# One row tile and two columns through the memory features' tile, with regrouped splits and a shared softmax scaling

## The chip, the cores and the metric

The kernel runs on one core of a Trainium2 chip. The metric is the device time of one execution in microseconds. The engines are TensorE (PE; its weight loads are PEld), VectorE (DVE), ScalarE (ACT), GpSimd (POOL) and SyncE (SP), which here only issues DMAs. Each engine works through a list of its own, in order.

## The reference

One layer of a streaming encoder over a prompt of 2048 rows and 128 sample rows (8 streams of 16), width 1024. The rows are RMS-normalised and projected once; three groups of heads read the result, each result is gated, and one projection merges them:

```python
def _rmsnorm(x, g):
    xf = xf * lax.rsqrt(jnp.mean(xf * xf, axis=-1, keepdims=True) + EPS)
    return (xf * g.astype(jnp.float32)).astype(x.dtype)
...
    qa, ka, va, ga, qb, kb, vb, gb, qm, gm = _project(yp, g_pre[l], w_in[l])
    oa = _band_attention(...)      # A: 6 heads, own chunk of 64 rows and 8 chunks before
    ob = _band_attention(...)      # B: 6 query heads on 2 key heads, own chunk and 2 before, with sinks
    om = _attn_core(...)           # M: 4 heads into 256 memory tokens
    yp = _merge(yp, oa, ga, ob, gb, om, gm, w_out[l], g_post[l])
...
def _merge(x, oa, ga, ob, gb, om, gm, w_out, g_post):
    o = jnp.concatenate([oa * jax.nn.silu(ga), ob * jax.nn.silu(gb), om * jax.nn.silu(gm)], axis=-1) @ w_out
    return x + _rmsnorm(o, g_post)
```

The sample rows do the same with cached keys and values. The new keys and values are outputs too.

## The kernel before

**Precision.** A float32 product is made of three products of a rounded part and a residual: ACT rounds a value (`split`, L238; `load_w`, L157; `split_mixed`, L961), DVE or POOL subtracts to get the residual (L239, L158, L962), and TensorE does three passes. So each weight tile (128x1024, through `wraw` to `whl`) costs a DMA, an ACT pass and a DVE or POOL pass, and every tile that a matmul reads does likewise.

**Groups.** The prompt is worked in four groups of 512 rows (g = 0 to 3); group 0 carries the 128 sample rows as well. Each group has two lanes of steps that are interleaved by hand-set costs: a dense lane (`DENSE`) and an attention lane (`ATTENTION`).

- `V`, `K`, `Pa`, `Pb`: projections of values, keys, and of query, key and gate of a pair of heads (`project_T`, L217, with 128x512 moving; `project_N`, L230, with 128x256 moving).
- `N0`: `next_scales(g + 1)`, the RMS factors of the next group's rows. `row_scales` loads four tiles of 128 rows (L175) and squares each in place on ACT (L176) with a running sum; `row_factors` turns the four factors into a 128x512 tile by small matmuls (L187), kept in `rsn`. The row tiles come from the pool tag "x", which has two buffers, and which the samples' cached values (`vta`, `vtb`), the residual rows `xr` and the gains use too.
- `L0`: `load_rows(g + 1)` loads the next group's rows by columns (eight of 128x512), scales each (L194, DVE) and splits it (L238 on ACT, L239 on DVE for even and POOL for odd columns) into `xn`. For group 1 each column is a tile of its own under the tag "xk", two buffers, 256 KB a load (L199). For later groups the columns from 2 on come in pairs (L479).
- `Q0`, `Q1`: query and gate of the next group's memory heads. They read all eight columns in order.
- `O0` to `O3`: the output projection of the group before, in quarters. `O0` first splits the gated features of each row tile (`split_mixed`, L961 on ACT and L962 on DVE) into `mixhl`.
- `F0`: `finish`, the last norm and the residual rows (L546, L547, L548).
- `M0`, `M1`, `Aa0` to `Aa2`, `Ab0` to `Ab2` and, in group 0, `Sa`, `Sb`: the attention of two memory heads, two A heads, two B heads, and of the samples. A head's part is `weigh` (scores, row minimum, exponential, reciprocal, scaling of the exponentials) and `combine` (transposes L277, `split`, the product with the values L290, `merge` L297 and L298, and after the second head `gate`, L688 on POOL).

**Features.** `mo` holds 8 feature columns of 128 for each of 5 row tiles: 0 to 2 from A, 3 to 5 from B, 6 and 7 from M. From group 1 on the memory heads' results (6 and 7) go into `mom`, a separate tile of 128 x 2 x 4 x 128, since `mo` still holds the group before. In group 0 `mom` is not written. Feature 2 comes from `Aa2`, the last attention step of each group.

**Order.** Python code emits instructions in the order of the two lanes. The framework then fixes each engine's list when the program is built: it allots buffers and takes what is ready first by a timeline that it works out from expected durations. On the chip these lists are not reordered. `tc.issue_after(last["w"])` keeps a DMA behind the latest weight load in SP's list.

Of the kernel before, what the change touches and what calls it, by code (L numbers as in the profile page):

```python
# [9 lines left out]
F32 = mybir.dt.float32  # L10
# [3 lines left out]
ALU = mybir.AluOpType  # L14
# [4 lines left out]
D = 1024  # L19
KB = D // 128  # L20
# [45 lines left out]
def encoder_step(ctx, tc, x_p, x_s, xT0, xT, mem, memT, wt, wm, g_pre, g_mem, g_post, rel_rev, sink,  # L66
# [3 lines left out]
    pe, act, dve, pool, sp = nc.tensor, nc.scalar, nc.vector, nc.gpsimd, nc.sync  # L70
# [4 lines left out]
    xp = ctx.enter_context(tc.tile_pool(name="xp", bufs=2))  # L75
# [14 lines left out]
    mo = cst.tile([128, 5, KB, 128], F32, name="mo")  # L90
# [7 lines left out]
    mom = cst.tile([128, 2, 4, 128], F32, name="mom")  # L98
# [14 lines left out]
    mixhl = region(0, 5, 2, KB, 128)  # L113
# [33 lines left out]
    last = {}  # L147
# [18 lines left out]
        dve.tensor_scalar(rstd[:, :n], ss[:, :n], 1.0 / D, EPS, ALU.mult, ALU.add)  # L166
        pool.tensor_tensor(rstd[:, :n], rstd[:, :n], expo[:, :n], ALU.pow)

    def row_scales(rows):

        n = len(rows)
        st = stp.tile([128, 16], F32, tag="nst", name="nst", bufs=3)
        for i, src in enumerate(rows):
            xt = xp.tile([128, D], F32, tag="x", name="xt")
            sp.dma_start(out=xt, in_=src)  # L175
            act.activation(xt, xt, AF.Square, accum_out=st[:, i:i + 1])  # L176
        rms_scale(st, n, st[:, 8:16])
        return st[:, 8:8 + n]

    def row_factors(rstd, n):  # L180

        rb = p_mm.tile([128, 512], F32, tag="mm", name="rb") if n == 4 else p_s.tile([128, 1024], F32, tag="s", name="rb")
        dg = xp.tile([128, 640], F32, tag="xk", name="dg", bufs=2)
        for i in range(n):
            d = dg[:, i * 128:(i + 1) * 128]
            dve.tensor_scalar(d, ident, rstd[:, i:i + 1], None, ALU.mult)
            pe.matmul(rb[:, i * 128:(i + 1) * 128], ones, d, start=True, stop=True)  # L187
        return rb
# [268 lines left out]
    def group_rows(g):  # L457
        return [x_p[g * GR + i * 128:g * GR + (i + 1) * 128] for i in range(4)] + ([x_s] if g == 0 else [])

    def next_scales(g):  # L460
        rb = row_factors(row_scales(group_rows(g)), 4)
        act.activation(rsn, rb, AF.Copy)

    def zero_rows(q):

        for h in range(2):
            pool.memset(q[64 - 64 * h:128 - 64 * h, 2 + h].bitcast(F32), 0.0)

    def load_rows(g):
        if g == 1:  # L470
            zero_rows(qslots[2])
        t = {}

        def column(k):
            if g == 1 or k in (0, 1):
                return loaded(xT[g - 1, :, k], 512)
            if k % 2 == 0:
                t[0] = xp.tile([128, D], F32, tag="x", name="xk2")
                sp.dma_start(out=t[0].rearrange("p (k r) -> p k r", k=2), in_=xT[g - 1, :, k:k + 2])  # L479
            return t[0][:, 512 * (k % 2):512 * (k % 2) + 512]  # L480

        scaled(rsn, column, gpre, xnT[1], 512)
# [40 lines left out]
    def gains():  # L523
        t = xp.tile([128, D], F32, tag="x", name="gpost")
        sp.dma_start(out=t, in_=g_post.partition_broadcast(128))
        return t, stp.tile([128, 32], F32, tag="pst", name="pst", bufs=2)
# [112 lines left out]
    for g in range(NG):  # L639
# [53 lines left out]
        def attn_m(pr, q, Q, G):  # L693
            f = 6 + pr
            held = {}

            def weigh(h):
                s = p_s.tile([128, 1024], F32, tag="s", name="sm")
                st = stp.tile([128, 16], F32, tag="st", name="stm")
                for i in range(4):  # L700
                    scores(s, q, h, i * 128, [(i * 256, mK[:, pr], 0, 256)])
                dve.tensor_reduce(st[:, 0:4], s.rearrange("p (a b) -> p a b", b=256), AX.X, ALU.min)
                held[h] = []
                for i2 in range(2):
                    sb = sbp.tile([128, 640], F32, tag="sb", name="sbm")
                    for i in (2 * i2, 2 * i2 + 1):
                        act.activation(sb[:, (i % 2) * 256:(i % 2) * 256 + 256], s[:, i * 256:(i + 1) * 256], AF.Exp,
                                       bias=st[:, i:i + 1], scale=-1.0, accum_out=st[:, 4 + i:5 + i])
                    dve.reciprocal(st[:, 8 + 2 * i2:10 + 2 * i2], st[:, 4 + 2 * i2:6 + 2 * i2])
                    for i in (2 * i2, 2 * i2 + 1):  # L710
                        c = sb[:, (i % 2) * 256:(i % 2) * 256 + 256]
                        dve.tensor_scalar(c, c, st[:, 8 + i:9 + i], 0.5, ALU.mult, ALU.mult)
                    held[h].append(sb)
                yield 950

            def combine(h):
                if h == 0:
                    held["sums"] = cp_.tile([128, 512], F32, tag="sums", name="sums")
                o = p_o.tile([128, 512], F32, tag="o", name="om")
                for i2 in range(2):  # L720
                    pt = transposed_p([held[h][i2][:, i * 256 + j * 128:i * 256 + (j + 1) * 128]
                                       for j in range(2) for i in range(2)])
                    yield 440
                    attend(o, [(mV[:, pr, j, 128 * h:128 * h + 128], pt, 256 * j, 256, 256 * i2) for j in range(2)],
                           i2 == 0)
                    yield 470
                merge(o, h, 0, held["sums"], 512)
                if h:
                    gate(f, 0, 512, held["sums"], G)

            return [(weigh(h), combine(h)) for h in range(2)]


# [226 lines left out]
        def split_mixed(dst, i, fs, src):  # L960
            act.activation(dst[:, i, 0, fs], src, AF.Copy)  # L961
            dve.tensor_tensor(dst[:, i, 1, fs], src, dst[:, i, 0, fs].bitcast(F32), ALU.subtract)  # L962

        def out_quarter(c):

            nrt = 5 if g == 1 else 4
            if c == 0:
                turn["m"] = 1
                for i in range(nrt):
                    if g == 1:  # L970
                        split_mixed(mixhl, i, slice(0, KB), mo[:, i])
                    else:
                        split_mixed(mixhl, i, slice(0, 6), mo[:, i, :6])
                        split_mixed(mixhl, i, slice(6, KB), mom[:, :, i])
                kept["post"] = gains()
            ws = [weights("o", c, r) for r in range(2)]
            for i in range(nrt):
                yield from project_out(ws, c, i, *kept["post"])
            if c == 3:
                turn["m"] = 0  # L980
# [15 lines left out]
        def dense():  # L996
            for step in DENSE[g].split():
                yield after(step)
                what, j = step[:-1], int(step[-1])
                if what == "O":  # L1000
                    yield from out_quarter(j)
                elif what == "E":
                    yield from early_quarters()
                elif what == "V":
                    vsm.extend((yield from block_v(vslots[2 * j:2 * j + 2], j)))
                elif what == "K":
                    kept["ksm"] = yield from block_k(3, ks[3], bkT, bkTs, 128)
                    if g:
                        pool.tensor_copy(keys[:, :, 0:128], bctx[0].bitcast(F32))
                elif what == "N":  # L1010
                    next_scales(g + 1)
                elif what == "L":
                    load_rows(g + 1)
                elif what == "X":
                    load_ctx(j)
                elif what == "C":
                    kept["bctx"] = keep_context()
                elif what == "F":
                    finish(g - 1, [4] if j else range(4), kept["post"][1])
                elif what == "Q":  # L1020
                    q, Q = yield from block_q(g + 1, 6 + j)
                    new_qg.append((q, Q, (yield from block_g(g + 1, 6 + j))))
                elif what == "Pa":
                    pa[j] = yield from project_a(j, ks[j], vslots[j])
                elif what == "Pb":
                    pb[j] = yield from project_b(j)
                done.add((g, step))
# [46 lines left out]
        while any(lanes):  # L1074
            ready = [lanes[k] is not None and done.issuperset(waits[k]) for k in range(2)]
            assert any(ready), (g, waits)
            k = 0 if ready[0] and (not ready[1] or spent[0] <= PACE * spent[1]) else 1
# [13 lines left out]
        room = [t.rearrange("p (a b) -> p a b", a=2) for t in (sh[:, 5376:7424], xn[:, 8192:])]  # L1091
        wl = weights("last")
        ws = [load_w(wt[W_AT["o", EARLY + j // 2, j % 2]], (room + [None] * 2)[j]) for j in range(4)]
        gpost, st = gains()
        for i in range(4):
            split_mixed(mixlast, i, LAST, mo[:, i, LAST])
            xt = xp.tile([128, D], F32, tag="x", name="xr") if i % 2 else wrawp.tile([128, D], F32, tag="wraw", name="xr")
# [154 lines left out]
```

## Time and profile before

| what | value |
|---|---|
| median of 3 runs | 1156.48 us (1156.46 to 1157.14) |
| the profiled execution's own time | 1157.69 us |
| its span, first to last instruction | 1155.6 us |
| mean granted TensorE clock | 0.993 |
| PE / PEld busy | 1116.2 / 1015.6 us |
| DVE / ACT / POOL busy | 799.2 / 729.0 / 314.9 us |
| DMA | 162.63 MB, mean 141 GB/s |

A row of a timeline has the start in us, the duration, the engine, the line, the operation, what it writes and reads, the shape, and a count when several are merged; a bracket at the end holds the engine's idle time before it and what ended that. Matmuls overlap each other, so their durations in a merged row add up to more than the row's time.

### The profile page before, as it was taken

Reading aid. Unit: us, or ns where it says so; the run is one execution under the profiler, and the core shown is the slowest. Engines: PE = TensorE matmul, PEld = TensorE weight load, DVE = VectorE, ACT = ScalarE, POOL = GpSimd, SP = SyncE. Lnnn points to the kernel's source line nnn. Section 1 sums busy time; section 2 is a strip of 40 time slices with the busy share of each in tenths; the row PEclk is TensorE's granted clock in tenths of the full one; section 3 lists DMA queues with packets and bytes.
Section 4 is the critical chain, followed back from the end, with each engine's and each line's share of the span. In section 5 each row is a group of like instructions: output and inputs, shape, how many; then the busy total and the mean of one; then the engine's idle time right before and its main releaser. Section 6 shows DMA issues by size and latency. Waiting matters only on the chain.

```text
span 1155.6 us, 20990 instructions
## 1 busy us (share of the span) xinstructions
PE 1116.2 (97%) x7794; PEld 1015.6 (88%) x7794; DVE 799.2 (69%) x1859; ACT 729.0 (63%) x1688; POOL 314.9 (27%) x259
## 2 busy tenths in 40 slices
PE   7999999998899999999999999999999999999897
PEld 6989898997689988988889988988889988898797
DVE  7758666677684447669888337779887347587965
ACT  7747557566574556658776455667776456577762
POOL 4212111111321552221431441221421541212320
PEclk9999999999999999999999999999999999999999
DMA  8584655324622594233321394233321483242213
GB/s 281 157 261 170 203 173 178 100 96 143 224 74 74 180 331 159 93 122 100 111 73 38 119 384 165 93 123 97 113 73 38 145 315 104 74 124 73 83 56 109
DMA packets 62620, 162.63 MB, mean 141 GB/s; under 512 B 8492, under 2 KB 19762, under 8 KB 62520
## 3 DMA queue, kind: packets, MB, share of 16 engines
q1 hardware_dynamic: 58776, 151.87, 39.1%
q0 software_dynamic: 3744, 9.44, 2.8%
q8 instruction: 61, 1.00, 0.3%
q14 instruction: 39, 0.32, 0.1%
HBM read 140.16 MB, written 23.48 MB: 142 GB/s over the span
## 4 chain that ended last, share of the span: by engine, by line
PE 80%; DMA 7%; DVE 5%; ACT 3%; issue 2%; POOL 1%; SPq 1%; DVEq 0%; POOLq 0%; ACTq 0%
PE psT L217 34%; PE psN L230 21%; PE pt L277 6%; PE oa L290 4%; PE sa L271 4%; PE psT L569 3%; DMA xt<-in_x_p 2%; PE ob L290 2%; PE sm L271 1%; PE om L290 1%; PE ss L391 1%; DMA xk<-in_xT 1%; DMA skew_d<-e_d 1%; DMA wraw<-in_wt 1%; DVE sh L239 1%
## 5 line engine op out<-in xcount | busy, mean ns | idle before, releaser
L217 PE MATMUL psT<-xn,whl 128*128 128x512 f32 (+2 forms) x2256 | 495.8, 368 | 13.1 <-ACT whl L157 6.4
L217 PEld LDWEIGHTS psT<-xn,whl 128*128 128x128 f32 x2256 | 384.3, 191 | 69.8 <-ACT whl L157 6.6
L158 POOL TENSOR_TENSOR whl<-wraw,whl 128x1024 fp32r<-128x1024 f32 x63 | 151.7, 2407 | 320.1 <-ACT whl L157 281.0
L230 PE MATMUL psN<-whl,sh 128*128 128x256 f32 x1296 | 160.6, 282 | 2.4 <-DVE sh L962 2.1
L230 PEld LDWEIGHTS psN<-whl,sh 128*128 128x128 f32 x1296 | 155.3, 188 | 4.9 <-DVE sh L962 2.8
L157 ACT ACTIVATE whl<-wraw 128x1024 fp32r<-128x1024 f32 (+1 forms) x132 | 138.6, 1050 | 30.5 <-PE psN L230 15.0
L230 PE MATMUL psN<-whl,xn 128*128 128x256 f32 x1080 | 145.2, 283 | 0.8 <-DVE sh L239 0.8
L230 PEld LDWEIGHTS psN<-whl,xn 128*128 128x128 f32 x1080 | 134.3, 188 | 2.9 <-issue 1.4
L239 DVE TENSOR_TENSOR sh<-pt,sh 128x512 fp32r<-128x512 f32 (+2 forms) x206 | 123.4, 626 | 14.7 <-ACT sh L238 13.2
L238 ACT ACTIVATE sh<-pt 128x512 fp32r<-128x512 f32 (+2 forms) x206 | 104.8, 550 | 21.5 <-PE pt L277 14.6
L158 DVE TENSOR_TENSOR whl<-wraw,whl 128x1024 fp32r<-128x1024 f32 (+1 forms) x69 | 96.3, 1395 | 18.1 <-ACT whl L157 15.2
L810 ACT ACTIVATE sba<-sba,sta 128x640 f32<-128x640 f32 (+2 forms) x96 | 73.2, 762 | 45.3 <-DVE sta L808 44.5
L808 DVE CUSTOM_DVE_ANT_0 sba<-sa,nbA 128x640 f32<-128x640 f32 (+2 forms) x96 | 70.8, 737 | 34.5 <-PE sa L271 33.6
L688 POOL TENSOR_TENSOR mo<-sums,gr 128x256 f32<-128x256 f32 (+1 forms) x38 | 38.0, 1000 | 201.1 <-DVE sums L298 187.7
L290 PE MATMUL oa<-sh 128*128 128x256 f32 (+1 forms) x504 | 75.6, 279 | 4.2 <-ACT sh L238 2.5
L290 PEld LDWEIGHTS oa<-sh 128*128 128x128 f32 x504 | 69.0, 190 | 7.9 <-ACT sh L238 2.7
L277 PE MATMUL pt<-ident,sba 128*128 128x128 f32 x420 | 67.8, 278 | 0.4 <-DVE sh L239 0.4
L533 DVE TENSOR_TENSOR mo<-psN,gpost 128x256 f32<-128x256 f32 x52 | 21.9, 423 | 66.3 <-ACT junk L532 66.1
L271 PE MATMUL sa<-sh,qr 128*128 128x320 f32 (+2 forms) x240 | 51.7, 328 | 4.6 <-DVE sta L808 3.4
L894 ACT ACTIVATE sbb<-sbb,stb 128x256 f32<-128x256 f32 (+1 forms) x96 | 47.2, 494 | 11.8 <-DVE stb L892 11.3
L277 PEld LDWEIGHTS pt<-ident,sba 128*128 128x128 f32 x420 | 50.2, 142 | 3.8 <-DVE sh L239 0.9
L532 ACT ACTIVATE junk<-psN 128x256 bf16<-128x256 f32 x52 | 20.0, 386 | 52.8 <-PE psN L230 52.8
(289 smaller groups left out, 1663.3 us busy)
## 6 DMA issues: line engine op xcount, KB each, us to landing
wraw<-in_wt SPq DMA_DIRECT2D x128, 512.0 KB, 3.6
xr<-in_x_p SPq DMA_DIRECT2D x16, 512.0 KB, 5.0
nbA<-skew_d SPq DMA_DIRECT2D x48, 144.0 KB, 3.6
vta<-in_cva SPq DMA_DIRECT2D x12, 512.0 KB, 6.3
xt<-in_x_p SPq DMA_DIRECT2D x12, 512.0 KB, 7.0
out_y_p<-mo SPq DMA_DIRECT2D x12, 512.0 KB, 6.5
vctx<-sh SPq DMA_DIRECT2D x9, 512.0 KB, 4.8
kctx<-sh SPq DMA_DIRECT2D x9, 512.0 KB, 4.3
```

The lines of the kernel that those rows point to most:

```text
L157: act.activation(hl[:, 0, m], raw[:, m], AF.Copy)
L158: eng.tensor_tensor(hl[:, 1, m], raw[:, m], hl[:, 0, m].bitcast(F32), ALU.subtract)
L217: pe.matmul(ps[:, :n], w[:, a, k * 128:(k + 1) * 128], src[:, b, k, c0:c0 + n], start=(i == 0), stop=(i == 23))
L230: pe.matmul(ps[:, :256], stat(a, k), w[:, b, (k % 4) * 256:(k % 4 + 1) * 256], start=(k == ks[0] and i == 0), stop=(k == ks[-1] and i == 2))
L238: act.activation(hi, src, AF.Copy)
L239: eng.tensor_tensor(lo, src, hi.bitcast(F32), ALU.subtract)
L271: pe.matmul(out[:, c:c + n], q[:, part, qc:qc + 128], kt[:, h, kc:kc + n], start=part == h, stop=part != h)
L277: pe.transpose(pt[:, i * 128:(i + 1) * 128], b, ident)
L290: pe.matmul(o[:, oc:oc + w], v, pt[:, part, c:c + w], start=(first and i == 0), stop=(i == n - 1), skip_group_check=True)
L808: dve.tensor_tensor_reduce(sb[:, :nk], s[:, c0:c0 + nk], nb[h][:, 640 - nk:], 1.0, 3.0e38, ALU.add, ALU.min, st[:, e:e + 1])
L810: act.activation(sb[:, :nk], sb[:, :nk], AF.Exp, bias=st[:, e:e + 1], scale=-1.0, accum_out=st[:, 2 + e:3 + e])
L894: act.activation(dst, dst, AF.Exp, bias=st[:, i:i + 1], scale=-1.0, accum_out=st[:, 4 + i:5 + i])
```

## The change

Four edits in the functions above:

1. `row_scales` takes `room`. For group 1 the third of the four row tiles (i = 2) is loaded into `mom` and squared there; the other three use the "x" buffers as before.
2. `staged_rows` loads columns 4 and 5 of group 1's rows into `mom` in one DMA of 512 KB. It is issued in group 0 at the start of `Pa2`, behind the latest weight load. `load_rows(1)` reads these two columns from `mom`, scaled in place, and loads the other six as before.
3. In `attn_m` of groups 1 to 3 the scaling of the exponentials of row tiles 2 and 3 runs on POOL, that of tiles 0 and 1 stays on DVE.
4. `out_quarter(0)` splits the features in other pieces: for each row tile 6 and 7 (from `mom`, in groups 2 and 3), then 3 to 5 (3 to 7 in group 1), then 0 and 1; after all row tiles, feature 2 of each. Before, they were split as 0 to 7 in group 1, and as 0 to 5, then 6 and 7, later.

```diff
-    def row_scales(rows):
+    def row_scales(rows, room=None):
...
         for i, src in enumerate(rows):
-            xt = xp.tile([128, D], F32, tag="x", name="xt")
+            if room is not None and i == 2:
+                xt = room.rearrange("p a b c -> p (a b c)")
+            else:
+                xt = xp.tile([128, D], F32, tag="x", name="xt")
             sp.dma_start(out=xt, in_=src)
...
     def next_scales(g):
-        rb = row_factors(row_scales(group_rows(g)), 4)
+        rb = row_factors(row_scales(group_rows(g), mom if g == 1 else None), 4)
...
+    def staged_rows():
+
+        sp.dma_start(out=mom.rearrange("p (k a) b c -> p k (a b c)", k=2), in_=xT[0, :, 4:6])
...
         def column(k):
+            if g == 1 and k in (4, 5):
+                if k == 4 and False:
+                    staged_rows()
+                return mom.rearrange("p (k a) b c -> p k (a b c)", k=2)[:, k - 4]
...
-                        dve.tensor_scalar(c, c, st[:, 8 + i:9 + i], 0.5, ALU.mult, ALU.mult)
+                        eng = pool if g and i > 1 else dve
+                        eng.tensor_scalar(c, c, st[:, 8 + i:9 + i], 0.5, ALU.mult, ALU.mult)
...
                 for i in range(nrt):
-                    if g == 1:
-                        split_mixed(mixhl, i, slice(0, KB), mo[:, i])
-                    else:
-                        split_mixed(mixhl, i, slice(0, 6), mo[:, i, :6])
+                    if g > 1:
                         split_mixed(mixhl, i, slice(6, KB), mom[:, :, i])
+                    split_mixed(mixhl, i, slice(3, 6 if g > 1 else KB), mo[:, i, 3:6 if g > 1 else KB])
+                    split_mixed(mixhl, i, slice(0, 2), mo[:, i, 0:2])
+                for i in range(nrt):
+                    split_mixed(mixhl, i, 2, mo[:, i, 2])
...
                 elif what == "Pa":
+                    if g == 0 and j == 2:
+                        with tc.issue_after(last["w"]):
+                            staged_rows()
                     pa[j] = yield from project_a(j, ks[j], vslots[j])
```

## The prediction

> **What bounds the kernel now.** I read the page's parts 1 and 4 first, then windows over the span, then single engines where the windows fell short.
>
> ```profile
> PE 1116.2 (97%) x7794; PEld 1015.6 (88%) x7794; DVE 799.2 (69%) x1859; ACT 729.0 (63%) x1688; POOL 314.9 (27%) x259
> PE 80%; DMA 7%; DVE 5%; ACT 3%; issue 2%; POOL 1%; SPq 1%; DVEq 0%; POOLq 0%; ACTq 0%
> ```
>
> TensorE is busy 1116.2 of 1155.6 us and is 80% of the chain: only its idle time (39.4 us) and slow-clock time can be won. Windows say where these lie. Columns: stretch, length, PE, PEld, DVE, ACT, POOL busy, granted clock, DMA share, GB/s.
>
> ```profile
> 197.50:200.90 3.40, 1.24 (x11) 1.03 (x9) 0.49 (x2) 1.86 (x4) 0.48 (x1) 1.00 0.04 14
> 200.90:204.30 3.40, 2.98 (x9) 2.72 (x10) 3.23 (x9) 2.39 (x6) 2.26 (x2) 0.50 0.51 164
> 204.30:207.70 3.40, 3.40 (x12) 3.40 (x12) 1.38 (x3) 0.00 (x0) 0.65 (x1) 0.50 0.52 163
> ...
> 306.70:310.10 3.40, 1.85 (x32) 1.29 (x34) 0.44 (x3) 0.60 (x2) 0.00 (x0) 1.00 0.54 199
> 310.10:313.50 3.40, 3.40 (x23) 2.80 (x16) 3.32 (x10) 1.54 (x3) 1.00 (x1) 0.51 0.48 152
> ...
> 576.35:579.76 3.41, 2.11 (x17) 1.84 (x16) 2.98 (x6) 3.31 (x6) 2.39 (x1) 1.00 0.00 0
> 579.76:583.20 3.44, 3.35 (x14) 2.73 (x15) 3.38 (x7) 3.34 (x8) 0.00 (x0) 1.00 0.56 173
> ...
> 278.00:300.00 22.00, 16.05 (x132) 10.26 (x124) 17.66 (x53) 14.94 (x37) 7.39 (x11) 1.00 0.73 230
> 320.00:360.00 40.00, 40.00 (x294) 37.57 (x293) 28.50 (x53) 26.50 (x66) 7.92 (x8) 1.00 0.25 80
> 600.00:625.00 25.00, 23.35 (x197) 22.80 (x196) 22.59 (x49) 18.43 (x56) 2.71 (x4) 1.00 0.02 8
> ```
>
> Three places matter to this change: around 200 us, 278 to 313 us, and the start of groups 2 and 3 (600 to 625 us is the first). At 320 to 360 us TensorE has no idle time, so nothing is won there. A gap costs twice: after a stretch of 3.4 us with 1.85 us of PE work the clock is half for one stretch; after one with 1.24 us it is half for two. After 2.11 us it stays full.
>
> **The change, part by part.**
>
> **Third row tile into the memory tile (N0).** The squares of group 1's rows sit in ScalarE's queue, and each waits for its load:
>
> ```profile
> 182.91 1.06 ACT L176 ACTIVATE xt<-xt 128x1024 f32<-128x1024 f32 x1 [0.94 <-DMA xt<-in_x_p]
> 188.26 1.06 ACT L176 ACTIVATE xt<-xt 128x1024 f32<-128x1024 f32 x1 [2.14 <-DMA xt<-in_x_p]
> 192.90 1.06 ACT L176 ACTIVATE xt<-xt 128x1024 f32<-128x1024 f32 x1 [0.23 <-DMA xt<-in_x_p]
> 198.99 1.06 ACT L176 ACTIVATE xt<-xt 128x1024 f32<-128x1024 f32 x1 [2.21 <-DMA xt<-in_x_p]
> ...
> 184.09 0.33 SPq L175 DMA_DIRECT2D xt<-in_x_p  x1
> 194.07 0.33 SPq L175 DMA_DIRECT2D xt<-in_x_p  x1
> ...
> 201.22 0.58 PE L290 MATMUL oa<-sh 128*128 128x256 f32 x1 [2.48 <-ACT sh L238]
> ```
>
> Each load is issued just after the square before it (184.09 after 182.91+1.06): of the two "x" buffers only one turns, so four loads stand in line. The fourth square ends about 200 us, and the softmax part behind it (L238) is what PE waits 2.48 us for. With the third tile in `mom`, which nothing uses in group 0, three stand in line and the fourth is issued about one turn (4.6 to 5.3 us) earlier. ScalarE's waits are 0.94+2.14+0.23+2.21 = 5.52 us over four; at that mean (1.38) three cost 4.14. TensorE lost 2.48 of 5.52, so 3.04 were absorbed; 4.14-3.04 leaves 1.10 us idle. That is less than the 1.30 us (3.41-2.11) that the clock survived, so the two half-speed stretches, worth half of 6.8 = 3.4 us, go as well. Gain 2.48-1.10+3.4 = 4.8. Ends: 0 (the wait only moves along) and 5.9. I take 4.8, the end it is nearest to by these rows. What is late next: the second load, now beside the third.
>
> The Trainium skill (TensorE: Matmul & The Clock Gate, section "HAM oscillation — how this bites in real kernels") asks for no idle gap above about 3.4 us. By that rule a 2.48 us wait costs no clock, this term would be 1.4 and the sum 4.1 (1152.4 us). The trace disagrees: the half clock follows gaps of 2.48 us and less.
>
> **Columns 4 and 5 staged in `mom` (L0).** The row columns come in pairs through two "xk" buffers:
>
> ```profile
> 279.09 0.82 SPq L199 DMA_DIRECT2D xk<-in_xT  x2
> 285.81 1.42 SPq L199 DMA_DIRECT2D xk<-in_xT  x2
> 296.09 0.97 SPq L199 DMA_DIRECT2D xk<-in_xT  x2
> 303.88 1.48 SPq L199 DMA_DIRECT2D xk<-in_xT  x2
> ...
> 282.27 0.75 DVE L194 SCALAR_TENSOR_TENSOR xk<-xk,gpre,rsn 128x512 f32<-128x512 f32 x1 [0.64 <-DMA xk<-in_xT]
> 312.71 0.69 DVE L239 TENSOR_TENSOR xn<-xk,xn 128x512 fp32r<-128x512 f32 x1
> 302.92 0.73 PE L217 MATMUL psT<-xn,whl 128*128 128x512 f32 x2 [0.39 <-ACT xn L238]
> 309.45 1.31 PE L427 MATMUL so<-vta,spT 128*32 128x128 f32 x28 [1.37 <-DMA vta<-in_cva]
> ```
>
> One 512 KB load issued before Pa2 (one SP issue more there, of the 0.33 us that the L175 rows show, behind the last weight; the third square, which frees `mom`, is then past: even now it ends at 194 us, two B projections before Pa2) replaces two of 256 KB here. Columns 6 and 7 take the turn at 296.09 in place of 303.88, so the first projection of group 1 has its last columns some 8 us sooner and can fill the waits at 302.92 and 309.45; if the latter falls below 1.3 us the half-speed stretch at 310 (1.7 us) goes. At best 0.39+1.37+1.7 = 3.5. Against it: DVE now scales columns 4 and 5 (2 x 0.75) between 278 and 296 us, where it is 17.66 of 22 us busy and the attention parts that PE waits on queue behind it; with one residual on DVE (0.69) 2.2 us worse at the other end. I take 1.5, toward the gain: the last columns are what is late.
>
> **Splits regrouped, half of the memory softmax's scaling on POOL.**
>
> ```profile
> 609.67 2.88 PE L230 MATMUL psN<-whl,sh 128*128 128x256 f32 x23 [0.46 <-DVE sh L962]
> 616.59 3.80 PE L230 MATMUL psN<-whl,sh 128*128 128x256 f32 x30 [1.01 <-DVE sh L962]
> 868.47 2.98 PE L230 MATMUL psN<-whl,sh 128*128 128x256 f32 x23 [0.42 <-DVE sh L962]
> 874.67 4.77 PE L230 MATMUL psN<-whl,sh 128*128 128x256 f32 x37 [0.33 <-ACT sh L961]
> ...
> 602.08 0.95 DVE L962 TENSOR_TENSOR sh<-mo,sh 128x768 fp32r<-128x768 f32 x1
> 609.53 0.42 DVE L962 TENSOR_TENSOR sh<-mom,sh 128x256 fp32r<-128x256 f32 x1
> L712 DVE TENSOR_SCALAR sbm<-sbm,stm x64: 336/350/1493, 83.0 to 886.1; 128x256 f32<-128x256 f32 x64
> 296.55 0.51 POOL L814 TENSOR_SCALAR sba<-sba,sta 128x256 f32<-128x256 f32 x1
> L158 POOL TENSOR_TENSOR whl<-wraw,whl 128x1024 fp32r<-128x1024 f32 x63 | 151.7, 2407 | 320.1 <-ACT whl L157 281.0
> ```
>
> After the last gate only feature 2 (128 wide) is left. From 0.95 for 768 and 0.42 for 256, 0.10 per 100 columns: 384 cost 0.55 and 128 cost 0.28. The last piece falls from 0.95 to 0.28, so the four waits (0.46+1.01+0.42+0.33 = 2.2 us) can close. The price is 0.55+0.42+0.28-0.95 = 0.30 us more DVE for each of 4 tiles, 1.2 us a group (ScalarE about as much). In group 1 the extra pieces, five tiles, meet the 40.00 of 40.00 window and cost nothing; if that cover went, three pieces for one would cost about 0.3 us a tile there too.
>
> Of the scalings, 2 of 4 for each head half, 4 head halves a group, 3 groups: 24 leave DVE (24 x 0.35 = 8.4 us, 2.8 a group, more than the 1.2 added) and cost POOL 24 x 0.51 = 12.2. POOL is 2.71 of 25 us busy at 600. Behind each in POOL's queue stand gates and weight residuals; PE's transposes wait for the scaled half. Ends: 2.2 won, or the POOL rival's loss below; I take 1.2, about half, since DVE names three of the four waits and POOL's answer is 0.16 us slower each time.
>
> **Sum:** 4.8+1.5+1.2 = 7.5 us. The profiled execution took 1157.69 (span 1155.6), so 1150.2; the median of the three runs is 1.2 below it, so 1149.0.
>
> **Rivals.** (a) The N0 wait stays. The scheduler sets ScalarE's order from expected loads: if it moves the fourth square up by the turn that the load gains, PE waits as long as now, only earlier. For it: the second square waited 2.14 us with a single load in flight. Against: a chain of three has one overrun less. Gain 1.5+1.2 = 2.7: 1153.8.
>
> (b) POOL and DVE get in each other's way.
>
> ```profile
> 335.46 1.22 DVE L158 TENSOR_TENSOR whl<-wraw,whl 128x1024 fp32r<-128x1024 f32 x1
> 399.10 2.64 DVE L158 TENSOR_TENSOR whl<-wraw,whl 128x1024 fp32r<-128x1024 f32 x1 [0.27 <-ACT whl L157]
> 398.24 2.41 POOL L547 TENSOR_TENSOR mo<-mo,xr 128x1024 f32<-128x1024 f32 x1
> ```
>
> The same DVE subtraction takes 1.22 us alone and 2.64 beside a POOL addition. If each moved scaling holds DVE up for its 0.51, DVE gets 8 x 0.51 = 4.1 back for 2.8 taken, with the splits 2.5 us more a group; in groups 2 and 3, where DVE is 22.59 of 25 us busy, PE pays that: 4.8+1.5-5.0 = 1.3 gained, 1155.2. The Trainium skill (Advanced Engine Details and Errata, section "Mode Summary") says that VectorE's second SBUF port is shared with GPSIMD and the two block each other; by that rule this rival is the likely one, and the three rows agree for the large tiles.
>
> (c) Slower: POOL's order. A scaled half queues behind a weight residual of 2.41 us, and PE, in order, waits at the transposes. It decides once the 12 head halves lose more than (7.5+2.3)/12 = 0.82 us each; at half a residual (1.2) the loss is 14.4-7.5 = 6.9, 1163.4. For it: POOL is strictly one list, and PE has idle time in these stretches already. Against: POOL's load there, 2.71 of 25 and 7.92 of 40 us.
>
> **Chances.** Forecast 0.46, (a) 0.20, (b) 0.18, (c) 0.13, more than forecast (all best ends, 5.9+3.5+2.2 = 11.6, 1144.9) 0.03. This measurement can tell about 0.2%, 2.3 us: faster is below 1154.2, slower above 1158.8. (a) lies 0.4 inside faster, so I give it 0.14 there and 0.06 to same: faster 0.63, same 0.06+0.18 = 0.24, slower 0.13. Range 1145 to 1158, from all best ends to just past (b); outside are (c) and a little of the rest. The forecast's own range is 1146 to 1153.
>
> **What would show it.** N0: ScalarE's fourth square about 194 us, PE's gap at 201 below 1.3 us, clock 1.00 throughout 197 to 208. L0: three pairs of L199 issues, the last near 296; no half clock at 310. Starts of groups 2 and 3: L962 no longer releases PE, and POOL names no wait of L277. I am wrong if PE waits for POOL's scaling by 0.82 us a time, or if the half-clock stretches return elsewhere because all later work shifts against them.

## The result, and the profile after

The changed kernel takes 1148.45 us (median of 6 runs, 1146.96 to 1152.17), the kernel before 1156.38 beside it: ratio 0.9938, 95% interval 0.9918 to 0.9959. The profiled execution took 1148.7 us, its span is 1146.8. Predicted were 1149.0 us (a gain of 7.5); measured is a gain of 7.9. The total came out; the experiments show that two of its three terms, and how they add up, did not.

The page of after, busy times and the shares of the chain that ended last:

```profile
PE 1114.0 (97%) x7794; PEld 1012.7 (88%) x7794; DVE 792.2 (69%) x1861; ACT 733.4 (64%) x1714; POOL 326.0 (28%) x283
PE 85%; DMA 5%; DVE 4%; ACT 3%; issue 2%; SPq 0%; POOL 0%; DVEq 0%; POOLq 0%; ACTq 0%
```

TensorE is idle 32.8 us of the span (1146.8-1114.0) where it was 39.4 (1155.6-1116.2). Windows of after, columns as in the prediction:

```profile
200.90:204.30 3.40, 3.23 (x23) 3.03 (x22) 3.34 (x10) 2.86 (x6) 1.08 (x1) 1.00 0.07 27
276.35:279.76 3.41, 2.13 (x23) 1.11 (x23) 3.20 (x13) 2.28 (x8) 1.20 (x3) 1.00 0.31 84
279.76:283.17 3.41, 2.53 (x14) 2.13 (x18) 1.98 (x10) 2.15 (x9) 0.29 (x2) 0.50 0.92 283
...
310.10:313.50 3.40, 3.40 (x18) 2.83 (x18) 3.29 (x8) 3.28 (x9) 1.21 (x1) 1.00 0.75 230
...
300.00:320.00 20.00, 20.00 (x137) 15.81 (x126) 12.61 (x31) 13.86 (x27) 6.58 (x8) 1.00 0.57 202
320.00:360.00 40.00, 37.71 (x289) 35.49 (x289) 26.27 (x59) 23.76 (x74) 10.92 (x15) 1.00 0.17 54
600.00:625.00 25.00, 24.62 (x209) 24.22 (x208) 21.60 (x46) 19.07 (x59) 8.39 (x11) 1.00 0.09 28
```

The half clock at 201 and at 310 is gone, and 600 to 625 has 24.62 us of PE work where it had 23.35. But the half clock is at 280 now, and 320 to 360, full before, has lost 2.3 us. The timeline names the waits there and at the starts of groups 2 and 3:

```profile
326.80 1.21 PE L274 MATMUL sm<-mK,xn 128*128 128x256 f32 x8 [0.23 <-DVE sta L820]
330.52 0.59 PE L233 MATMUL psN<-whl,sh 128*128 128x256 f32 x2 [0.64 <-ACT sh L973]
340.47 1.84 PE L233 MATMUL psN<-whl,sh 128*128 128x256 f32 x8 [1.20 <-DVE sh L974]
...
607.02 0.38 PE L233 MATMUL psN<-whl,sh 128*128 128x256 f32 x1 [0.31 <-ACT sh L973]
861.88 1.92 PE L233 MATMUL psN<-whl,sh 128*128 128x256 f32 x14 [0.36 <-DVE sh L974]
```

(L973 and L974 are the two lines of `split_mixed`, before L961 and L962.) And the row tiles, in after's timelines of SP, ACT and PE:

```profile
14.49 0.33 SPq L178 DMA_DIRECT2D mom<-in_x_p  x1
16.03 0.33 SPq L156 DMA_DIRECT2D wraw<-in_wm  x1
...
26.51 1.05 ACT L179 ACTIVATE mom<-mom 128x1024 f32<-128x1024 f32 x1
...
L179 ACT ACTIVATE xt<-xt x3: 1061/1062/1064, 186.4 to 196.4; 128x1024 f32<-128x1024 f32 x3
...
30.27 0.71 PE L190 MATMUL rb<-dg,ones 128*128 128x128 f32 x4 [1.60 <-DVE dg L189]
202.46 0.46 PE L190 MATMUL rb<-dg,ones 128*128 128x128 f32 x2 [0.17 <-DVE dg L189]
295.03 0.97 SPq L202 DMA_DIRECT2D xk<-in_xT  x2
```

(In the line with `x3` stand the least, median and longest duration in ns, then the first and last start.) The first line is the surprise. The third row tile is not loaded at 180 us beside its fellows, but at 14.49 us, and squared at 26.51, in the start of the kernel. Nothing in `mom` holds it back, and the framework takes what is ready first.

**Where the time went.** No edit touches the weight loads, so ScalarE's 132 weight roundings (into `whl`, L157) come in the same order in every version; the start of the n-th of them is a milestone. Each entry is its start less that of before, in one profiled execution each (the columns are named by its time before):

| execution | 7th (41) | 22nd (170) | 28th (234) | 31st (294) | 40th (368) | 52nd (452) | 64th (561) | 70th (627) | 106th (909) |
|---|---|---|---|---|---|---|---|---|---|
| after, first | +1.63 | +3.35 | -1.66 | -0.44 | -1.72 | -3.13 | -2.81 | -6.12 | -7.58 |
| after, second | +1.58 | +4.41 | -0.83 | +0.07 | -1.74 | -3.15 | -2.84 | -6.12 | -7.86 |
| row tile in x again | +0.31 | +1.64 | +0.75 | +1.38 | +0.23 | -1.18 | -0.87 | -4.17 | -5.85 |
| row tile loaded late | -0.01 | +1.75 | -4.71 | +0.61 | -1.20 | -2.61 | -2.30 | -5.60 | -7.34 |
| splits as before | +1.11 | +2.30 | -2.88 | -2.89 | -0.26 | -1.67 | -1.67 | -1.60 | -2.14 |
| row edits alone | +1.65 | +1.75 | -3.36 | -3.29 | +0.29 | -1.46 | -1.46 | -1.45 | -2.51 |

After loses 1.6 us in the start and wins 5.0 to 5.2 at 200 us. Of that little is left at 294, about 1.3 to 1.8 come by 368 and 1.4 by 452. Then 3.3 are won at group 2's start and 1.5 to 1.7 around group 3's. What the column of the 22nd shows is mostly the execution, not the edit. Row tile in x again and late edits alone have before's lists of PE, ACT and DVE up to 210 us, and their 22nd rounding is 1.64 and 1.37 us late; row tile loaded late and the last two versions of the next section have them up to 165 us and then one square of 1.06 us, and are 1.75, 3.86 and 6.72 late.

### The profile page after: what moved, and what is told of

It is laid out like the page before. It is cut to its first block, busy times and chain, and to the rows that moved or that the text cites. A ratio compares the mean times of both kernels' runs of the same rounds, so it can differ in the third digit from the quotient of the medians.

```text
span 1146.8 us, 21056 instructions
## 1 busy us (share of the span) xinstructions
PE 1114.0 (97%) x7794; PEld 1012.7 (88%) x7794; DVE 792.2 (69%) x1861; ACT 733.4 (64%) x1714; POOL 326.0 (28%) x283
## 4 chain that ended last, share of the span: by engine, by line
PE 85%; DMA 5%; DVE 4%; ACT 3%; issue 2%; SPq 0%; POOL 0%; DVEq 0%; POOLq 0%; ACTq 0%
PE psT L220 37%; PE psN L233 21%; PE pt L280 6%; PE oa L293 4%; PE sa L274 4%; PE psT L580 3%; PE ob L293 2%; DMA wraw<-in_wt 2%; PE om L293 1%; PE sm L274 1%; DVE whl L158 1%; PE ss L394 1%; DMA skew_d<-e_d 1%; PE so L430 1%; DVE sh L242 1%
## 5 line engine op out<-in xcount | busy, mean ns | idle before, releaser
L233 PE MATMUL psN<-whl,sh 128*128 128x256 f32 x1296 | 165.2, 282 | 2.8 <-DVE sh L974 1.6
L157 ACT ACTIVATE whl<-wraw 128x1024 fp32r<-128x1024 f32 (+1 forms) x132 | 138.5, 1049 | 28.6 <-PE psN L233 12.5
```

Of the source, the lines that this page charges most:

```text
L157: act.activation(hl[:, 0, m], raw[:, m], AF.Copy)
L233: pe.matmul(ps[:, :256], stat(a, k), w[:, b, (k % 4) * 256:(k % 4 + 1) * 256], start=(k == ks[0] and i == 0), stop=(k == ks[-1] and i == 2))
```

## The experiments

Each kernel ran beside the kernel before; ratios are to that. Differences between two versions are of medians unless the ratios are named; the median of the kernel before itself moved by up to 0.75 us between the series of the table.

| kernel | median us | before | ratio | 95% interval |
|---|---|---|---|---|
| after, again | 1147.76 | 1155.19 | 0.9937 | 0.9921 to 0.9952 |
| after, row tile in x | 1150.68 | 1155.19 | 0.9959 | 0.9946 to 0.9972 |
| after, row tile loaded late | 1147.43 | 1155.19 | 0.9940 | 0.9924 to 0.9955 |
| after, group 1 split as before | 1152.50 | 1155.19 | 0.9980 | 0.9967 to 0.9993 |
| after, columns not staged | 1149.30 | 1155.63 | 0.9955 | 0.9938 to 0.9971 |
| after, scaling all on DVE | 1148.28 | 1155.63 | 0.9953 | 0.9935 to 0.9972 |
| after, all groups split as before | 1157.53 | 1155.63 | 1.0024 | 1.0009 to 1.0039 |
| before, late edits alone | 1153.80 | 1155.63 | 0.9994 | 0.9975 to 1.0012 |
| before, row edits alone | 1157.46 | 1154.88 | 1.0020 | 1.0003 to 1.0037 |
| after, last piece 384 wide | 1156.19 | 1154.88 | 1.0015 | 0.9999 to 1.0031 |
| late row tile, last gate on DVE | 1149.26 | 1154.88 | 0.9959 | 0.9945 to 0.9973 |
| late row tile, four pieces in group 1 | 1151.30 | 1155.10 | 0.9966 | 0.9951 to 0.9981 |

**The changed kernel again**, no edit.

> The changed kernel again, beside the others of this series. Both theories: 1148.5 us (1147 to 1152), its profile as the first one: a PE gap of 1.60 us at 30.27 us and of 1.45 us at 96.47 us, and the n-th weight rounding 3.35 us later than before by 170 us. If these are only the luck of one execution, the profile of this one has them elsewhere or smaller.

The time repeats, and a loss of 1.6 us in the start too, but in another form. In this execution there is no gap at 30 us, but a half-clock stretch at 26.65, and the gap at 97 is 2.89 us with one behind it.

**The third row tile in an "x" buffer again.**

```diff
-        rb = row_factors(row_scales(group_rows(g), mom if g == 1 else None), 4)
+        rb = row_factors(row_scales(group_rows(g)), 4)
```

> The changed kernel with all four row tiles in the x buffers again. Theory 'loaded at the start': since nothing holds the load of the third tile back, it is issued at 14.49 us, some 160 us before its place, and its square sits among the start's; the profile of the changed kernel is 3.35 us late by 170 us and wins 5.0 us at 200, so the edit is worth 1.7 us net: 1150.1 us here, the gaps at 30 and 96 us gone, the 2.48 us wait at 201 us and its half-clock stretch back. Theory of the prediction: the edit is worth 4.8 us, and the 3.35 us come from something else: 1153.3 us, gaps at 30 and 96 us still there.

```profile
202.93 0.58 PE L293 MATMUL oa<-sh 128*128 128x256 f32 x1 [2.55 <-ACT sh L241]
```

The wait is back, the start is as before (+0.31 at the 7th rounding). 2.9 us by the medians, 2.5 by the ratios (0.0022 of 1155 us): less than the predicted 4.8, more than 1.7. Up to 212 us the lists of PE, ACT and DVE are those of before, and yet there is a gap of 1.18 us at 94 us: that part of after's lag at 170 us varies between executions and is not the edit's. The 1.6 us in the start are the edit's only in part. Of the executions that kept the full clock around 26 us, all four with the early load (after, group 1 split as before, scaling all on DVE, all groups split as before) have the gap of 1.60 or 1.61 us at 30 us and are 1.11 to 1.63 us late at the 7th rounding; the five without it have no such gap and are at most 0.74 late. But where the half clock comes at 26 us, nothing of the early load is left to see: four executions with it are 1.31 to 1.65 late, and one with the load late (four pieces in group 1) is 1.80 late.

**The load of the third row tile kept behind the latest weight load.**

```diff
-            sp.dma_start(out=xt, in_=src)
+            if room is not None and i == 2:
+                with tc.issue_after(last["w"]):
+                    sp.dma_start(out=xt, in_=src)
+            else:
+                sp.dma_start(out=xt, in_=src)
```

> The changed kernel with the load of the third tile kept behind the latest weight load in SP's list (as the staged columns are). Theory 'loaded at the start': the load goes to about 165 us, the gaps at 30 and 96 us go, the gap at 201 us stays closed: 3.3 us less, 1145.1 us (1143 to 1147). Rival: three loads near each other at 165 to 190 us queue as before, the wait at 201 us returns at about half (1 to 2.5 us, with or without half clock): 1146 to 1150. Theory of the prediction (start not to blame): 1148.5.

```profile
158.92 0.61 SPq L180 DMA_DIRECT2D mom<-in_x_p  x1
...
284.28 0.65 PE L284 MATMUL pt<-ident,sbb 128*128 128x128 f32 x2 [2.44 <-DVE sbb L919]
296.16 3.30 PE L224 MATMUL psT<-xn,whl 128*128 128x512 f32 x13 [1.54 <-ACT whl L157]
```

```profile
274.09:277.50 3.41, 1.60 (x15) 0.98 (x15) 3.34 (x14) 2.28 (x10) 0.62 (x3) 1.00 0.36 106
277.50:280.92 3.42, 3.32 (x18) 1.82 (x17) 1.03 (x4) 2.56 (x10) 0.12 (x1) 0.50 0.89 259
280.92:284.33 3.41, 0.97 (x8) 0.49 (x4) 3.33 (x9) 0.90 (x2) 1.54 (x1) 1.00 0.67 218
```

The load moves to 158.92, the start's loss is gone (-0.01), the 28th rounding comes 4.71 us early: all as the theory said. And the time stays (1147.43 against 1147.76). In the profiled execution the stretch of 274 to 297 us took all of it: three windows at half clock (from 277.51 and from 284.33) and two larger gaps (2.44 and 1.54 us), +0.61 by the 31st rounding, though from 166 us on its lists are after's own. In the second execution of after the same stretch had no half clock. That it takes the gain every time is not shown; that the total does not gain 3 us is.

**Group 1's features in one piece again, groups 2 and 3 in the new pieces.**

```diff
+                    if g == 1:
+                        split_mixed(mixhl, i, slice(0, KB), mo[:, i])
+                        continue
```

> The changed kernel with group 1's features split as before in one piece of eight, groups 2 and 3 in the new pieces. Theory 'pieces cost group 1': the PE waits at 326.8, 330.5 and 340.5 us (0.23+0.64+1.20 = 2.1 us) go: 1146.4 us. Rival (the prediction's words, the pieces cost nothing there): the waits come from the order of the lists around L0, they stay and the time is 1148.5; or the waits go and come back as waits on the old pieces (L973, L974) of the same size.

```profile
339.70 0.30 PE L280 MATMUL pt<-ident,sbm 128*128 128x128 f32 x1 [3.06 <-DVE sbm L724]
```

The theory failed with the opposite sign: 4.7 us slower, with PE waits of 0.97, 0.83, 3.06 and 1.21 us at 325 to 359 us instead of 0.23, 0.64 and 1.20. The pieces do not cause group 1's waits, they make them shorter.

**Columns 4 and 5 through "xk" again** (the branch on columns 4 and 5 in `column` and the call of `staged_rows` at `Pa` removed).

> The changed kernel (1147.8 us) with columns 4 and 5 of group 1's rows loaded as the others, through the xk buffers. Theory of the prediction: the staged columns are worth 1.5 us (0 less than 3.5): 1149.3 us, four pairs of L202 issues, the last near 302 us, PE waits at 303 and 309 us back (0.39 and 1.37 us). Rival 'given back before 294 us': the stretch of 275 to 295 us takes whatever is won before it, and the gain of the earlier columns is lost in half-clock stretches: within 0.7 us of 1147.8.

```profile
301.57 0.33 PE L436 MATMUL spt<-ident,ssb 128*128 128x128 f32 x1 [0.78 <-DVE ssb L433]
305.89 0.41 PE L430 MATMUL so<-vta,spT 128*32 128x128 f32 x4 [0.93 <-ACT sba L818]
...
319.26 7.41 PE L220 MATMUL psT<-xn,whl 128*128 128x512 f32 x24 [2.02 <-DVE gr L625]
...
320.00:360.00 40.00, 40.00 (x284) 37.44 (x283) 27.16 (x54) 23.99 (x72) 10.91 (x13) 0.96 0.20 65
```

1.5 us slower by the medians, as the prediction had it, 2.1 by the ratios, though the intervals overlap. Six waits, 4.7 us in all, stand between 301 and 320 us. After has none there; this kernel in turn has none between 320 and 430.

**The scaling all on DVE** (`eng = dve`).

> The changed kernel (1147.8 us) with all of the memory softmax's scaling on DVE again. Theory of the prediction: DVE gets 2.8 us a group more, against 1.2 of splits; the waits at the starts of groups 2 and 3 (0.46, 1.01, 0.42, 0.33 us before) come back in part: 1149 to 1150 us. Rival (b), POOL and DVE get in each other's way: 1145 to 1147, since the pairs on POOL took 0.93 us each. Rival 'order alone': the lists differ in 56 of 7523 matmuls only, so within 0.7 us of 1147.8.

0.5 us slower by the medians, with intervals that overlap widely: undecided.

**All groups split as before** (the four lines of the diff's `-` side).

> The changed kernel (1147.8 us) with the features split as before in all groups. Theory of the prediction: the pieces are worth 2.2 us at the starts of groups 2 and 3 and nothing in group 1: 1150.0 us. Theory from the kernel with group 1's old splits (1152.5 us, PE waits of 0.97, 0.83, 3.06 and 1.21 us at 325 to 359 us): the pieces are worth 4.7 us in group 1 and 2.2 us beyond: 1154.7 us.

9.8 us slower, slower even than the kernel before. Where: 560 to 626 us has 62.91 us of PE work against after's 65.17 (rows below), and 324 to 360 only 29.96 of 36.00 against 33.71.

**The late edits alone, on the kernel before.**

> The kernel before (1155.2 us) with only the regrouped splits and the shared scaling. Theory of the prediction: 1.2 us: 1154.0 us. Theory from the two profiles (the n-th weight rounding moves by 3.3 us more between 560 and 627 us, by 1.4 between 850 and 896, by 3.9 between 1075 and 1110, of which the last depends on a clock stretch of 1.7): the late edits are worth 4.7 to 7 us: 1148.2 to 1150.5 us. Group 1's start tells where the waits at 330 and 340 us come from: if they are here too, they are the pieces' or the scaling's; if not, they need the staged columns or the row tile.

```profile
324.00:360.00 36.00, 36.00 (x282) 34.70 (x281) 23.66 (x46) 21.80 (x67) 10.01 (x12) 1.00 0.19 60
```

A gain of 1.8 by the medians, 0.7 by the ratio, within its interval of nothing. But group 1's start is full: the waits at 326 to 340 us come neither from the pieces nor from POOL. The profiled execution was the fastest of the twelve (1149.4 us, clock 0.995; the others 0.985 to 0.991), so what these edits win in groups 2 and 3 was there (-1.34 to -4.65 from the 64th to the 70th rounding). That the other executions lost much of it in half-clock stretches is likely by their clocks; they have no profile that shows where.

**The row edits alone, on the kernel before.**

> The kernel before (1155.6 us) with the third row tile and the two columns in the memory features' tile, and neither the regrouped splits nor the shared scaling. Theory of the prediction: its two terms, 4.8+1.5 = 6.3 us: 1149.3 us. Theory 'the cover is gone': what the rows win by 320 us (the waits at 201, 303 and 309 us and their half-clock stretches) is given back at 324 to 359 us, since the projections that ran beside group 0's splits are over too early; as in the kernel without regrouped splits, PE waits of about 0.98, 0.82, 3.05 and 1.21 us there: 1155.6 to 1158 us, no faster than before.

```profile
319.33 1.87 PE L220 MATMUL psT<-xn,whl 128*128 128x512 f32 x7
324.65 1.16 PE L293 MATMUL oa<-sh 128*128 128x256 f32 x8 [0.98 <-DVE sums L301]
326.62 0.58 PE L233 MATMUL psN<-whl,sh 128*128 128x256 f32 x1 [0.82 <-ACT sh L973]
...
339.70 1.81 PE L274 MATMUL sm<-mK,qr 128*128 128x256 f32 x8 [2.41 <-ACT sbm L718]
343.97 1.21 PE L233 MATMUL psN<-whl,sh 128*128 128x256 f32 x8 [1.17 <-DVE sh L974]
```

Slower than before by 0.2%, where the prediction's two terms would be 6.3 us faster. The kernel before has in that place:

```profile
328.07 5.14 PE L217 MATMUL psT<-xn,whl 128*128 128x512 f32 x21
```

That projection came late, since its columns did, and TensorE worked on it while ACT and DVE split group 0's features. With the columns staged, the last projection (the row at 319.33) is over by 321.2 us, in after by 324.4, and nothing covers the splits: the four waits above, 5.4 us, and half-clock stretches at 326 and 340. What the rows win until 320 us is given back by 360. In all eleven profiles with staged columns PE waits 2.1 to 6.3 us in all between 322 and 362 us (in waits of over 0.2 us), in the three without (before, columns not staged, late edits alone) not at all.

**The last piece 384 wide instead of 128.**

```diff
-                    split_mixed(mixhl, i, slice(0, 2), mo[:, i, 0:2])
                 for i in range(nrt):
-                    split_mixed(mixhl, i, 2, mo[:, i, 2])
+                    split_mixed(mixhl, i, slice(0, 3), mo[:, i, 0:3])
```

> The changed kernel (1147.8 us) with the last piece of each row tile 384 wide (features 0 to 2 after the last gate) instead of 128. Theory of the prediction (the size of the last piece is the gain): 384 cost DVE 0.55 and 128 cost 0.28, so 0.27 more for 4 or 5 tiles a group, over three groups up to 3.5 us: 1149 to 1151 us, waits on L973 and L974 at 331, 341, 607 and 862 us each 0.3 to 1 us longer. Rival (the gain comes from taking features 3 to 7 out ahead of the last gate, the last piece's size matters little): within 0.7 us of 1147.8.

Both theories miss: 8.4 us slower. The split residuals alone (L974 or L962 on DVE) between 580 and 597 us, ahead of group 2's last gate, and all engines from 560 to 626, in turn for the kernel before, after, all groups split as before, and this one:

```profile
580.00:597.00 17.00, 0.43 (x1) 1.00 0.28 93
560.00:626.00 66.00, 62.39 (x426) 56.42 (x425) 56.67 (x111) 48.34 (x112) 18.49 (x18) 1.00 0.20 65
```

```profile
580.00:597.00 17.00, 4.71 (x6) 1.00 0.26 84
560.00:626.00 66.00, 65.17 (x458) 59.87 (x458) 57.42 (x115) 50.41 (x122) 22.28 (x25) 1.00 0.24 76
```

```profile
580.00:597.00 17.00, 0.43 (x1) 1.00 0.19 64
560.00:626.00 66.00, 62.91 (x434) 57.15 (x433) 54.38 (x103) 48.43 (x113) 20.97 (x26) 1.00 0.21 65
```

```profile
580.00:597.00 17.00, 0.98 (x2) 1.00 0.19 63
560.00:626.00 66.00, 62.53 (x417) 56.76 (x416) 52.99 (x103) 47.21 (x111) 21.08 (x24) 0.97 0.20 65
```

Six pieces run ahead of the gate in after, one or two in the others, and after has 2.3 to 2.8 us more PE work in the 66 us. As far as these rows show, what the pieces bring here is to run in DVE's idle time before the gate; a price by the width of the last one does not reach 8.4 us. Why the framework also leaves the pieces of features 3 to 5 behind when the last one is 384 wide is not settled: compared place by place in the two profiles, 1250 of 7794 matmuls use other tiles than in after, and this execution has a half-clock stretch at 599.83 that after has not. So this run changes more than a width, and does not isolate the cause.

**The last A heads' gate on DVE, row tile loaded late** (in `gate`, `dve if f == 2 else pool`).

> The changed kernel with the third tile's load kept behind the latest weight load (1147.4 us) and the last A heads' gate (feature 2) on DVE instead of POOL. The two waits at 330 and 340 us end on a chain of that gate on POOL (1.31 and 0.97 us), ACT's split (0.51) and DVE's residual (0.48). Theory 'the gate is on the path': a 256-wide product on DVE takes about 0.43, so each of the two waits shortens by 0.5 to 0.9 us, and those at 607 and 862 us close: 1.2 to 2 us less, 1145.4 to 1146.2 us. Rival: DVE's list is full there, the gate queues behind a weight residual of 1.22 us: within 0.7 us of 1147.4, or 1 us slower.

```profile
331.60 1.17 PE L284 MATMUL pt<-ident,sbm 128*128 128x128 f32 x4 [1.27 <-DVE sbm L728]
354.74 5.51 PE L237 MATMUL psN<-whl,sh 128*128 128x256 f32 x43 [1.72 <-DVE mo L548]
```

The gate takes 0.42 on DVE instead of 0.97 to 1.31, the waits at 330 and 340 on L973 and L974 go, and one of 0.64 us on POOL (L830) and two of 1.27 and 1.72 us on DVE take their place: 1.8 us slower than row tile loaded late, with intervals that overlap.

**Group 1 in four pieces, row tile loaded late** (6 and 7 and 3 to 5 apart in all groups).

> The changed kernel with the third tile's load kept behind the latest weight load (1147.4 us), and group 1's features 3 to 7 split as 6 and 7, then 3 to 5, as in the later groups. Theory 'pieces ahead of the last gate win' (six residuals stood at 580 to 597 us in the changed kernel, one in the kernels that lose 2.8 us there): in group 1's list two more residuals now stand ahead of that gate, of 0.4 to 0.6 us each, so the waits at 326.8, 330.5 and 340.5 us (2.1 us) shrink by about 1 us: 1146.4 us. Rival: five more residuals on DVE at 0.14 us each and their copies on ACT where both are late: the wait at 340 us grows by up to 0.7 us: 1147.4 to 1148.1 us.

3.9 us slower than row tile loaded late by the medians, 3.0 by the ratios: both theories miss. The wait at 330 us shrinks (0.64 to 0.24), and waits of 1.44 (ACT, L722), 0.67 and 1.67 us (DVE, L978 and L548) appear behind it. Its profiled execution was the slowest of seven and late long before group 1 (6.72 us at the 22nd rounding, with before's lists up to 169 us), so the milestones of what follows say little. No version tried is measurably faster than the change itself.

## Why the prediction was right, and where it was not

**The total** was right by 0.6 us, partly by chance: the terms were 4.8, 1.5 and 1.2; undoing the parts one by one costs 2.9, 1.5 and 9.8 (splits) with 0.5 (scaling). They sum to 14.7, not to 7.9, and the two halves alone bring -2.6 and +1.8 (by the ratios -2.3 and +0.7, the latter within its interval of nothing). The failing step is the sum itself: it took the parts as independent.

**N0.** The mechanism was right: three loads in line, the last square ends at 197.4 in an execution that is 3.4 us late, PE's gap is 0.17 us, the clock stays 1.00 from 197 to 208, and 5.0 us are won there against 4.8. What failed is that `mom`, "which nothing uses in group 0", was read only as room and not as freedom to go at any time: the load left SP's list at 180 us for 14.49. The price, up to 1.6 us in the start where no half-clock stretch hides it, stands in no term; with the load kept late the total is the same (1147.43 against 1147.76). And the 3.4 us of half clock were taken from one execution as if they came in each: without the edit the same place wins 0.9 us between the 22nd and 28th rounding when 3.4 us at half clock follow the wait (row tile in x again) and 3.7 when none do (late edits alone, +1.37 to -2.33). By removal the term is 2.5 to 2.9, net of its price in the start, against the 4.8 forecast: it was mis-sized. The gap-length rule that the prediction quoted from the Trainium skill (TensorE: Matmul & The Clock Gate, section "HAM oscillation — how this bites in real kernels") gave 1.4; the runs lie between the two. Rival (a) is out.

**L0.** The net was as said, in the form said: three pairs, the last issued at 295.03, no half clock at 310, and DVE's scalings of columns 4 and 5 ran at 210.4 us, far from where they could hurt. But the cost that it does have was looked for at 278 to 296 us, and it lies at 324 to 359.

**Splits and scaling.** The failing sentence is that "nothing is won" at 320 to 360 us and that the pieces "cost nothing" in a window of 40.00 of 40.00. That window was full because of the late projection, which the change's own other part removes. The prediction did ask what happens "if that cover went", but did not see that its own L0 takes it away, and priced the loss at 0.3 us a tile against the new pieces. With the cover gone the old pieces leave 5.4 to 6.3 us of waits, the new ones 2.1. In groups 2 and 3 the term was mis-sized: 1.2 forecast, at most 2.2. The milestones have 3.3 us at group 2's start, where both kernels with the old pieces win nothing, and 1.5 to 1.7 around group 3's, of which the old pieces show 0.5 to 1.1 too. So the pieces bring about 4 there, since not only the named waits close: in the kernel before there is also a wait on a pair's gate (L618), which every kernel with the old pieces keeps and after has not.

```profile
579.85 5.17 PE L217 MATMUL psT<-xn,whl 128*128 128x512 f32 x21 [1.39 <-DVE gr L618]
```

The forecast that L962 no longer releases PE in groups 2 and 3 held but for 0.36 us at 861.88; POOL releases no transpose in the changed kernel, so rival (c) is out. Rival (b) is out as a cause that decides: without POOL's share the kernel is not faster by more than the interval allows.

## What to carry to other kernels

Ask of a load that gets a free buffer what still holds it back; if nothing does, it moves as far forward as the planner sees it ready, and it can cost time there (here a wait of 1.6 us in some executions, and nothing measurable in the total). A fully busy window is a cover that belongs to the work in it: before a term is set to nothing there, check that no other part of the change takes this work away. And measure the parts both ways, one removed and one alone: here neither half alone brings a gain clear of the noise, and together they bring 0.6%.

## What the runs showed of the hardware

The half-clock stretches of one execution start on a fixed grid. In the clock records their starts lie whole multiples of 3.413 us apart: 200.91, 310.13 and 1088.37 before (32 and 260 steps), 279.75 and 1081.88 after (235 steps). Another execution of the same kernel has another phase. Waits of 0.47, 0.25 and 1.14 us before 277.57, 278.36 and 280.34 us were followed by a half clock in after's first execution, which lost 3.4 us there; the same three, 0.8 us later, cost nothing in its second, which lost at 27 and 98 instead. The Trainium skill (TensorE: Matmul & The Clock Gate, section "Part 1: The HAM clock gate") describes such a free-running window of some 3.4 us; the grid agrees with that.

The prediction's rule (half clock after 1.85 us of PE work in a window, none after 2.11), on which the 1.30 us in its N0 term rest, does not hold on the grid either. There 1.60 us was followed by a half clock, but so was 2.13 (the row at 276.35 of after), and 1.87 (late edits alone, at 314.59) was not:

```profile
314.59:318.01 3.42, 1.87 (x13) 1.41 (x11) 3.42 (x8) 3.37 (x7) 3.20 (x4) 1.00 0.01 2
```

So PE's busy time alone does not decide it. In the second execution of after the half clock at 26.65 follows a window that is busy throughout:

```profile
23.24:26.65 3.41, 3.41 (x30) 3.41 (x29) 3.41 (x7) 2.60 (x8) 0.00 (x0) 1.00 0.83 269
26.65:30.06 3.41, 3.41 (x17) 3.34 (x15) 2.70 (x8) 3.41 (x8) 1.38 (x1) 0.50 0.78 256
```

```profile
23.32 1.17 PE L525 MATMUL ss<-ones,sq 128*128 128x2 f32 x10
24.61 1.17 PE L525 MATMUL ss<-ones,sq 128*128 128x2 f32 x10
```

Of that window 2.34 us are matmuls two columns wide. Every execution has this pair of rows, at another place on its grid. In five of the fourteen all 2.34 us fall into one window, and each of these five has the half clock behind it; in the other nine no window holds more than 2.10 us of them, and none has it. That these matmuls count for less than their time fits all fourteen; by how much, no run here shows. The lists do not decide it: up to 165 us the version with four pieces, which has the half clock at 26.95, and the kernel before, which has none there, run the same lists of PE, ACT and DVE.
